# Start of a two-layer hybrid block: all of x loaded first, on the queue of the modulation weights, with the first dense weights between the two modulation vectors and x stored behind the modulation

## The chip, the cores and the metric

The kernel runs on one core of one Trainium2 chip. The metric is the device time of one execution in microseconds (us). The engines are named as the profile names them: PE (TensorE, the matmuls), PEld (its weight loads), DVE (VectorE), ACT (ScalarE), POOL (GpSimd) and SP (SyncE, here only a queue from which transfers are issued). SPq and ACTq are the queues on which SP and ACT issue transfers.

## The reference

Two layers work on 512 latent tokens and 256 context tokens of 1024 channels. Each begins with a normalization whose result is scaled and shifted by vectors computed from the conditioning input, and one wide input projection:

```python
def reference(x, c, ctx, c_ctx, ada_w, ada_b, norm1_w, norm2_w, w_in, w_out, ...):
    for l in range(DEPTH):
        mod_x = jnp.split((jax.nn.silu(c) @ ada_w[l] + ada_b[l])[:, None, :], N_MOD, axis=-1)
        mod_c = jnp.split((jax.nn.silu(c_ctx) @ ada_w[l] + ada_b[l])[None, None, :], N_MOD, axis=-1)
        hx = modulate(rmsnorm(x, norm1_w[l]), mod_x[0], mod_x[1])
        hc = modulate(rmsnorm(ctx, norm1_w[l]), mod_c[0], mod_c[1])
        mix_x, mix_c = token_mixing(hx, hc, w_in[l], ...)
        x = x + mod_x[2] * (mix_x @ w_out[l])
        x = x + mod_x[5] * channel_mlp(modulate(rmsnorm(x, norm2_w[l]), mod_x[3], mod_x[4]), ...)
        ...
    return rmsnorm(x, final_norm_w)
```

`token_mixing` multiplies by `w_in` and runs four groups of heads on the columns: a gated delta rule, windowed attention, a gated MLP over chunks, and a bidirectional mLSTM.

## The kernel before, in words

Everything is float32. The 768 tokens (context first) lie along the free axis: `X[k]` is a tile of 128 channels by 768 tokens, k = 0 to 7. Each dense matmul is made of three (`hhi*whi`, `hlo*whi`, `hhi*wlo`), for which ACT rounds a weight block to `whi`, DVE makes the rest `wlo`, and likewise `hhi` and `hlo` of the activations.

The start, up to the first dense matmul, does this. ACT issues the loads of the six blocks of 128 tokens (`xs`, 512 KB each, line 400) and takes their sums of squares (`jk`); PE transposes them (`xps`, line 406), and DVE and ACT copy the transposes to `X` (lines 184 and 412). SP issues the loads of the modulation weights (`adw`, line 323, 512 KB each, eight for each vector, in five buffers); PE multiplies them into `adaps`. Two vectors, n = 0 (shift) and n = 1 (scale), are needed at the start. `ada_end` copies a finished sum to `adas` on ACT, has PE turn it (`adat`) and DVE add the bias (`mod`). `params` loads a row of parameters (`prow`) and gate constants (`tokp`). `modulated` computes `sc` from the scale vector, then for each k on DVE `hy`, on ACT `hhi` and on DVE `hlo`. The first dense product (`gemm_pair`) works on two weight blocks together, 32 gate columns (two loads of 16 columns, 64 KB each) and 128 columns, both staged in `wst` by SP (line 491; two buffers) and split by `wsplit`. `X` is stored to DRAM (`xd`, line 628, eight transfers on ACT's queue) since its buffers are used for other things until the layer's residual.

The order of the instructions on each engine is not the order of the code: the framework's scheduler places each instruction by its own estimate of when it is ready. At the end of the layer's token mixing, a block named `mix0` (line 1513 on) weaves attention (`scl`, `scc`, `pT`, `pv`, `P`, `sq`), mLSTM (`W`, `wps`, `num`, `qk`, `hT`, `sT`, `den`, `hn`, `hs`, `lq`) and dense work, and is placed by such a simulated timeline too. After it the output projection begins with `mhi` and `mlo`, first of the tile `uu`.

Of the kernel before, what the change touches and what calls it, by code (L numbers as in the profile page):

```python
# [9 lines left out]
F32 = mybir.dt.float32  # L10
# [8 lines left out]
D = 1024  # L19
# [3 lines left out]
NP = NT // 128  # L23
DEPTH = 2
# [10 lines left out]
C_GQ, C_GK, C_GV, C_GZ, C_AB = 0, 256, 512, 768, 1024  # L35
C_SQ, C_SK, C_SV = 1040, 1296, 1424
C_MU, C_MV = 1552, 1808
C_LQ, C_LK, C_LV, C_LO, C_IF = 2064, 2320, 2576, 2832, 3088
# [104 lines left out]
def flow_kernel(ctx, tc, t, out, dbg=None, stop=None):  # L143
    nc = tc.nc
# [23 lines left out]
    def gi(name="gi"):  # L168
        return pg.tile([128, 512], F32, tag="gi", name=name)

    def go1(name="go"):
        return pg.tile([128, 512], F32, tag="go", name=name)
# [126 lines left out]
    lay, zp, tp = layer_pools()  # L299
    ldx = ExitStack()  # L300
    ld = ldx.enter_context(tc.tile_pool(name="ld", bufs=5))

    sg = ld.tile([128, 16], F32, name="csg", bufs=1)
    cv = ld.tile([128, 16], F32, name="cv", bufs=1)
# [14 lines left out]
    def ada_sum(l, n, pl, o):  # L319

        for k in range(8):
            st = pl.tile([128, 4, 256], F32, tag="adw", name="adw")
            nc.sync.dma_start(out=st, in_=t["ada_w"][l, 128 * k:128 * k + 128, 1024 * n:1024 * n + 1024]
                              .rearrange("p (g n) -> p g n", g=4))
            for g in range(4):
                mm(o[32 * g:32 * g + 32, 0:256], scT[:, k], st[:, g], start=(k == 0), stop=(k == 7))
        return o
# [67 lines left out]
    X = [xm.tile([128, NT], F32, tag="xm", name="x") for _ in range(8)]  # L395
    ss0 = per.tile([128, NP], F32, name="ss0")
    for p in range(NP):
        xs = ld.tile([128, D], F32, tag="xs", name="xs", bufs=6)
        src = t["ctx"][0, 128 * p:128 * p + 128] if p < 2 else t["x"][0, 128 * (p - 2):128 * (p - 2) + 128]
        nc.scalar.dma_start(out=xs, in_=src)  # L400
        jk = ld.tile([128, D], F32, tag="jk", name="jk", bufs=1)
        act_(jk, xs, AF.Square, accum_out=ss0[:, p:p + 1])
        for g in range(2):
            pt = ps("xps")
            for k in range(4):
                T.transpose(pt[:, 128 * k:128 * k + 128], xs[:, 128 * (4 * g + k):128 * (4 * g + k) + 128], ident)
            for k in range(4):
                xo = X[4 * g + k][:, 128 * p:128 * p + 128]
                if k % 2:
                    act_(xo, pt[:, 128 * k:128 * k + 128], AF.Copy)  # L410
                else:
                    V.tensor_copy(out=xo, in_=pt[:, 128 * k:128 * k + 128])

    nc.scalar.dma_start(out=cst[:, 128:], in_=t["consts"][:, 128:NPERM])


    prm = [per.tile([128, 128], F32, name=f"prm{l}") for l in range(DEPTH)]
    tokp = [per.tile([128, 44], F32, name=f"tokp{l}") for l in range(DEPTH)]

    def params(l, rows):  # L420
        nc.scalar.dma_start(out=rows[0:NR], in_=t["prow"][l])
        nc.scalar.dma_start(out=tokp[l], in_=t["tok"][l:l + 1].to_broadcast([128, 44]))
        pt = gs("prmT")[:, 0]
        T.transpose(pt[:, 0:NR], rows[0:NR, :], ident[0:NR, 0:NR])
        V.tensor_copy(out=prm[l][:, 0:NR], in_=pt[:, 0:NR])

    ao = [ada_sum(0, 0, ld, go1("adaps")), ada_sum(0, 1, ld, gi("adaps"))]
    params(0, ld.tile([128, 128], F32, tag="prow", name="prow", bufs=1))
    for n in range(2):
        ada_end(0, n, ld, ao[n])  # L430

# [47 lines left out]
        return parts  # L479

    def wload(parts, order=None):
        st = wst.tile([128, 8, 128], F32, tag="wst", name="wst")
        o = 0
        for src in parts:
            n = src.shape[1]
            sv = src.rearrange("(k p) n -> p k n", p=128)
            for i in (range(0, 8, 2) if order else (0,)):
                if order:
                    nc.sync.dma_start(out=st[:, i:i + 2, o:o + n], in_=sv[:, order[i]:order[i] + 2])
                else:  # L490
                    nc.sync.dma_start(out=st[:, :, o:o + n], in_=sv)
            o += n
        return wsplit(st, o)

    def gemm(parts, acts, segs, n=128, order=None, pb=None, w2=None):

# [103 lines left out]
    for l in range(DEPTH):  # L600
# [19 lines left out]
        def z3(name, dt=F32):  # L620
            return zp.tile([128, NT], dt, tag="z3", name=name, bufs=6)

        ahead = [wload([win[:, C_AB:C_AB + 16], win[:, C_IF:C_IF + 16]]), wload([win[:, C_GK:C_GK + 128]])]
        h = modulated(l, 0, ALL, nrm, tp)
        del nrm
        xd = dp.tile([8, 128, NT], F32, tag="xd", name="xd")
        for k in range(8):
            nc.scalar.dma_start(out=xd[k, :, ow], in_=X[k][:, ow])

        def temp(tag, w=GAP + 4):  # L630
            return tp.tile([128, GAP + 4], F32, tag=tag, name=tag, bufs=1 if tag == "tc" else 2)
# [881 lines left out]
        with tc.block(name=f"mix{l}", schedule_with_timeline_sim=True):  # L1513
            for _ in states():
                pass
            if l == 0:
                params(1, temp("tc")[:, 0:128])
            no = len(opairs)
            for j in range(2):
                gdn_norm(j)  # L1520
            weave((3.5 * no, swa()), (2 * no, mlstm()), (14, dense()))
            for j in range(2):
                mv = mix[6 + j][:, ow]
                tt(mv, mv, gz[j][:, ow], MUL)
# [112 lines left out]
```

## Time and profile before

| what | value |
|---|---|
| time, median of 3 runs (lowest to highest) | 1961.99 us (1960.19 to 1962.09) |
| the profiled execution | 1955.14 us |
| its span, first to last instruction | 1953.4 us |
| PE busy | 1874.8 us, 96% of the span |
| DVE, ACT busy | 1201.8 us, 757.4 us |

The profiled execution is 1.7 us longer than its span and 6.9 us below the median of the others. The profile cuts the span into slices in which each engine's busy share, the clock granted to TensorE (as a share of its full 2.4 GHz; 0.50 is 1.2 GHz) and the transfers' rate can be read; a chain of waits leads back from the last instruction.

### The profile page before, as it was taken

The numbers are of one execution on the slowest core, as the hardware profiler recorded it, in microseconds if no ns is written. First come the engines' busy times: TensorE is split into PE (matmuls) and PEld (weight loads), VectorE is DVE, ScalarE is ACT, GpSimd is POOL, SyncE is SP. The second block draws the span as 40 slices with busy tenths as digits, with TensorE's granted clock in tenths as the row PEclk, the third lists the DMA queues.
The fourth block names the chain that finished last, engine by engine and source line by source line (L and its number), as shares of the span: only waits on it lengthen the run. The fifth ranks groups of instructions, "written<-read, shape, count | busy, mean of one in ns | idle before, by whom it ended". The sixth has DMA issues, their size and how long they took to land.

```text
span 1953.4 us, 34015 instructions
## 1 busy us (share of the span) xinstructions
PE 1874.8 (96%) x14131; PEld 1536.4 (79%) x14131; DVE 1201.8 (62%) x2221; ACT 757.4 (39%) x1530; POOL 104.6 (5%) x169
## 2 busy tenths in 40 slices
PE   5999999999899999999999999999999999999998
PEld 3877778778777888888888878677777778888887
DVE  3978885666769557435535349798676754444443
ACT  4652343555524312313213236434255543333242
POOL 0021110000000000000000000211100000000001
PEclk8999999999799999999999999999999999999999
DMA  8321001121464345335433222210011323333332
GB/s 310 97 52 34 13 24 34 57 65 34 147 199 129 107 131 148 116 93 151 140 87 108 78 58 55 63 35 24 23 44 33 102 81 98 97 97 97 97 97 76
DMA packets 225955, 172.56 MB, mean 88 GB/s; under 512 B 19106, under 2 KB 208008, under 8 KB 225800
## 3 DMA queue, kind: packets, MB, share of 16 engines
q1 hardware_dynamic: 219424, 153.71, 26.6%
q10 hardware_dynamic: 4680, 10.64, 1.5%
q0 software_dynamic: 1696, 6.03, 0.9%
q8 instruction: 111, 1.82, 0.4%
q14 instruction: 44, 0.36, 0.1%
HBM read 163.02 MB, written 7.34 MB: 87 GB/s over the span
## 4 chain that ended last, share of the span: by engine, by line
PE 82%; DVE 9%; ACT 3%; DMA 3%; issue 1%; POOL 1%; DVEq 0%; ACTq 0%; SPq 0%; POOLq 0%
PE mm L181 64%; PE mmt L181 3%; PE num L181 1%; PE ops L181 1%; DMA wst<-w_in 1%; PE pv L181 1%; DVE wlo L187 1%; DVE Y L187 1%; PE adaps L181 1%; PE yt L181 1%; DVE kq L190 1%; PE t L181 1%; PE pT L1353 1%; DMA adw<-ada_w 1%; PE yps L181 1%
## 5 line engine op out<-in xcount | busy, mean ns | idle before, releaser
L184 ACT ACTIVATE whi<-wst 128x512 fp32r<-128x512 f32 (+1 forms) x388 | 241.9, 627 | 683.8 <-PE mm L181 628.8
L181 PE MATMUL mm<-hhi,whi 128*128 128x512 f32 (+3 forms) x1344 | 479.5, 362 | 11.7 <-ACT hhi L184 11.0
L181 PE MATMUL mm<-hlo,whi 128*128 128x512 f32 (+3 forms) x1344 | 479.3, 357 | 1.2 <-DVE hlo L190 1.1
L181 PE MATMUL mm<-hhi,wlo 128*128 128x512 f32 (+3 forms) x1344 | 476.3, 356 | 0.0
L187 DVE TENSOR_TENSOR wlo<-wst,whi 128x512 fp32r<-128x512 f32 (+1 forms) x388 | 265.7, 689 | 312.9 <-ACT whi L184 308.5
L181 PEld LDWEIGHTS mm<-hhi,whi 128*128 128x128 f32 (+1 forms) x1344 | 252.7, 189 | 55.2 <-ACT hhi L184 14.4
L181 PEld LDWEIGHTS mm<-hlo,whi 128*128 128x128 f32 (+1 forms) x1344 | 253.9, 189 | 38.0 <-DVE hlo L190 2.3
L181 PEld LDWEIGHTS mm<-hhi,wlo 128*128 128x128 f32 (+1 forms) x1344 | 253.2, 189 | 38.6 <-issue 1.5
L181 PE MATMUL mm<-fhi,whi 128*128 128x512 f32 (+1 forms) x784 | 275.9, 352 | 0.0
L181 PE MATMUL mm<-flo,whi 128*128 128x512 f32 (+1 forms) x784 | 275.8, 352 | 0.0
L181 PE MATMUL mm<-fhi,wlo 128*128 128x512 f32 (+1 forms) x784 | 274.5, 350 | 0.0
L190 DVE SCALAR_TENSOR_TENSOR x<-mm,mod,x 128x256 f32<-128x256 f32 (+1 forms) x122 | 79.6, 653 | 139.8 <-PE mm L181 139.7
L181 PEld LDWEIGHTS mm<-fhi,whi 128*128 128x128 f32 x784 | 148.3, 189 | 21.9 <-ACT r L184 0.8
L181 PEld LDWEIGHTS mm<-fhi,wlo 128*128 128x128 f32 x784 | 148.1, 189 | 19.7
L181 PEld LDWEIGHTS mm<-flo,whi 128*128 128x128 f32 x784 | 148.4, 189 | 19.1
L190 DVE SCALAR_TENSOR_TENSOR adacc<-adw,scT,adacc 128x1024 f32<-128x1024 f32 x84 | 105.9, 1282 | 28.0 <-DMA adw<-ada_w 27.9
L187 DVE TENSOR_TENSOR flo<-r,fhi 128x768 fp32r<-128x768 f32 (+1 forms) x64 | 52.6, 825 | 39.2 <-ACT fhi L184 39.1
L184 ACT ACTIVATE fhi<-r 128x768 fp32r<-128x768 f32 (+1 forms) x64 | 47.2, 740 | 65.9 <-DVE r L187 65.9
L181 PE MATMUL mm<-mlo,whi 128*128 128x512 f32 (+1 forms) x192 | 69.7, 363 | 1.3 <-DVE mlo L187 1.3
L181 PE MATMUL mm<-mhi,whi 128*128 128x512 f32 (+1 forms) x192 | 69.5, 362 | 0.4 <-ACT mhi L184 0.4
L181 PE MATMUL mm<-mhi,wlo 128*128 128x512 f32 (+1 forms) x192 | 68.8, 359 | 0.0
L184 ACT ACTIVATE r<-mm 128x256 f32<-128x256 f32 (+1 forms) x96 | 49.1, 515 | 32.2 <-PE mm L181 32.2
(406 smaller groups left out, 2712.1 us busy)
## 6 DMA issues: line engine op xcount, KB each, us to landing
wst<-mlp_w SPq DMA_DIRECT2D x128, 512.0 KB, 3.8
adw<-ada_w SPq DMA_DIRECT2D x96, 512.0 KB, 4.1
wst<-w_in SPq DMA_DIRECT2D x44, 512.0 KB, 3.7
wst<-w_out SPq DMA_DIRECT2D x64, 128.0 KB, 3.2
xd<-x ACTq DMA_DIRECT2D x8, 384.0 KB, 3.4
x<-xd POOLq DMA_DIRECT2D x8, 384.0 KB, 5.5
xs<-x ACTq DMA_DIRECT2D x4, 512.0 KB, 7.2
wst<-w_in SPq DMA_DIRECT2D x8, 256.0 KB, 3.2
```

What stands on the lines that cost most here:

```text
L181: T.matmul(o, lhsT=l, rhs=r, start=start, stop=stop)
L184: S.activation(out=o, in_=i, func=f, **kw)
L187: (eng or V).tensor_tensor(out=o, in0=a, in1=b, op=op)
L190: V.scalar_tensor_tensor(out=o, in0=a, scalar=s, in1=b, op0=op0, op1=op1)
L1353: T.transpose(o[:, 256 * i + 128 * g:256 * i + 128 * g + 128], Ps[g][:, 128 * (i0 + i):128 * (i0 + i) + 128], ident)
```

## The change

The six loads of context and x go to the front of SP's queue, ahead of the modulation weights. `prow`, `tokp` and the constants are issued at once on ACT's queue. The first two dense blocks are staged (`wstage`, the loading half of the former `wload`) between the loads of the two modulation vectors and split later. Before the eight stores of `X`, a transfer of eight numbers of the scale vector (`mod`) is written to the place they will overwrite, so that the stores come behind the modulation. `params` of layer 1 loads its rows where it did before, through the new `params_load`.

```diff
+    xin = []
+    for p in range(NP):
+        xs = ld.tile([128, D], F32, tag="xs", name="xs", bufs=6)
+        src = t["ctx"][0, 128 * p:128 * p + 128] if p < 2 else t["x"][0, 128 * (p - 2):128 * (p - 2) + 128]
+        nc.sync.dma_start(out=xs, in_=src)
+        xin.append(xs)
...
+    def params_load(l, rows):
+        nc.scalar.dma_start(out=rows[0:NR], in_=t["prow"][l])
+        nc.scalar.dma_start(out=tokp[l], in_=t["tok"][l:l + 1].to_broadcast([128, 44]))
+        return rows
+
+    prow = params_load(0, ld.tile([128, 128], F32, tag="prow", name="prow", bufs=1))
+    nc.scalar.dma_start(out=cst[:, 128:], in_=t["consts"][:, 128:NPERM])
+
+    def wstage(parts, order=None):
+
+        st = wst.tile([128, 8, 128], F32, tag="wst", name="wst")
...
+    def first_blocks(l):
+        win = t["w_in"][l]
+        return [[win[:, C_AB:C_AB + 16], win[:, C_IF:C_IF + 16]], [win[:, C_GK:C_GK + 128]]]
...
-        xs = ld.tile([128, D], F32, tag="xs", name="xs", bufs=6)
-        src = t["ctx"][0, 128 * p:128 * p + 128] if p < 2 else t["x"][0, 128 * (p - 2):128 * (p - 2) + 128]
-        nc.scalar.dma_start(out=xs, in_=src)
+        xs = xin[p]
...
-    ao = [ada_sum(0, 0, ld, go1("adaps")), ada_sum(0, 1, ld, gi("adaps"))]
-    params(0, ld.tile([128, 128], F32, tag="prow", name="prow", bufs=1))
+    params(0, prow)
+    ao = [ada_sum(0, 0, ld, go1("adaps"))]
+    staged = [wstage(x) for x in first_blocks(0)]
+    ao.append(ada_sum(0, 1, ld, gi("adaps")))
...
-        ahead = [wload([win[:, C_AB:C_AB + 16], win[:, C_IF:C_IF + 16]]), wload([win[:, C_GK:C_GK + 128]])]
+        ahead = [wsplit(*x) for x in staged] if l == 0 else [wload(x) for x in first_blocks(l)]
...
+        if l == 0:
+
+            nc.scalar.dma_start(out=xd[:, 0:1, 0].rearrange("k p -> p k"), in_=mod[0][0:1, 8:16, 0])
         for k in range(8):
             nc.scalar.dma_start(out=xd[k, :, ow], in_=X[k][:, ow])
```

What stands where changes on every engine at the start, and, since the scheduler runs again, in the last quarter of `mix0`. Three places matter below.

SP at the start of the program, before (`xs` is the input by tokens, `adw` the modulation weights, `wst` the staged dense weights):

```order
L197 DMA crow<-crow 16x128
L323 DMA adw<-ada_w 128x1024 x5
L491 DMA wst<-w_in 128x8x16
L323 DMA adw<-ada_w 128x1024 x11
L491 DMA wst<-w_in 128x8x16
L491 DMA wst<-w_in 128x8x128
```

The same place now:

```order
L197 DMA crow<-crow 16x128
L306 DMA xs<-ctx 128x1024 x2
L306 DMA xs<-x 128x1024 x4
L359 DMA adw<-ada_w 128x1024 x8
L330 DMA wst<-w_in 128x8x16 x2
L330 DMA wst<-w_in 128x8x128
L359 DMA adw<-ada_w 128x1024 x8
```

The input stands ahead of all modulation weights, and the three loads of the first dense weights, one of which stood between the first and two behind the last of them, stand between the vectors.

ACT at the end of the first dense product, before (`ta` is the copy of the product out of PSUM, `Re` a constant table):

```order
L184 ACTIVATE whi<-wst 128x512 x2
L184 ACTIVATE Re<-e__1150 64x512
L184 ACTIVATE hhi<-hy,mod_121 128x256
L184 ACTIVATE hhi<-hy,mod_121 128x512
L184 ACTIVATE ta<-mm 32x256
L184 ACTIVATE whi<-wst 128x512
L184 ACTIVATE ta<-mm 32x512
```

The same place now:

```order
L184 ACTIVATE hhi<-hy,mod_141 128x256
L184 ACTIVATE hhi<-hy,mod_141 128x512
L649 DMA xd<-x 128x768 x2
L184 ACTIVATE ta<-mm 32x256
L184 ACTIVATE ta<-mm 32x512
L184 ACTIVATE whi<-wst 128x512 x2
L184 ACTIVATE ta<-mm 128x256
```

The first two roundings of the next weight block, which stood ahead of the last `hhi`, stand behind two copies of the finished product; `Re` went to the start of the product, behind its first `hhi`.

DVE at the end of `mix0` and the start of the output projection, before:

```order
L187 TENSOR_TENSOR hs<-hs,ss 128x256
L1339 RECIPROCAL sm<-sm 128x2
L1342 TENSOR_SCALAR P<-P,sm 128x256 x2
L187 TENSOR_TENSOR lq<-lq,gz_4708 128x768
L187 TENSOR_TENSOR lq<-lq,gz_4709 128x768
L1364 COPY sq<-pv 128x128
L1513 UNCONDITIONAL_BRANCH
L649 TENSOR_SCALAR tokp_268<-tokp_268 128x8
L187 TENSOR_TENSOR mlo<-uu,mhi 128x768 x2
```

The same place now:

```order
L1385 COPY sq<-pv 128x128
L1504 TENSOR_REDUCE ss<-sq_6396 128x4
L187 TENSOR_TENSOR hs<-hs,ss 128x256
L1385 COPY sq<-pv 128x128
L187 TENSOR_TENSOR lq<-lq,gz_4709 128x768
L187 TENSOR_TENSOR lq<-lq,gz_4710 128x768
L1534 UNCONDITIONAL_BRANCH
L670 TENSOR_SCALAR tokp_126<-tokp_126 128x8
L187 TENSOR_TENSOR mlo<-uu,mhi 128x768 x2
```

The two products with the gate `gz` moved behind the last attention copy, to the end of the block.

## Rows read from the trace of the kernel before

**Rows 1.** The page: span of the profiled execution.

```profile
span 1953.4 us, 34015 instructions
```

**Rows 2.** Busy time by stretch (PE, PEld, DVE, ACT, POOL), then granted clock, DMA share, GB/s.

```profile
2.00:4.00 2.00, 0.26 (x1) 0.18 (x1) 1.15 (x8) 0.03 (x1) 0.00 (x0) 1.00 0.87 202
...
4.00:12.00 8.00, 4.39 (x24) 3.43 (x28) 1.60 (x8) 3.56 (x10) 0.00 (x0) 1.00 1.02 406
12.00:16.00 4.00, 4.00 (x41) 1.84 (x34) 1.03 (x5) 2.45 (x9) 0.00 (x0) 1.00 1.04 309
16.00:32.00 16.00, 9.58 (x73) 5.78 (x71) 3.02 (x11) 6.36 (x18) 0.00 (x0) 0.75 1.00 395
...
34.00:36.00 2.00, 2.00 (x19) 1.30 (x17) 0.00 (x0) 0.59 (x2) 0.00 (x0) 0.91 0.15 42
...
44.00:51.00 7.00, 4.80 (x15) 3.04 (x16) 6.93 (x14) 3.96 (x8) 1.52 (x5) 0.50 0.95 301
```

**Rows 3.** Timeline, 0 to 45 us, SP's queue: start, duration, what, count.

```profile
12.62 21.09 SPq L323 DMA_DIRECT2D adw<-ada_w  x11
33.75 1.09 SPq L491 DMA_DIRECT2D wst<-w_in  x2
```

**Rows 4.** Waits of SP's queue to 43 us: total us, times, longest.

```profile
SPq L323 <- PE adaps L181: 17.8, 7, 5.6
```

**Rows 5.** Transfers issued before 43 us: count, size each, median us to landing.

```profile
adw<-ada_w SPq DMA_DIRECT2D x16, 512.0 KB, 7.0
xs<-x ACTq DMA_DIRECT2D x4, 512.0 KB, 7.2
...
cst<-consts ACTq DMA_DIRECT2D x1, 512.0 KB, 7.6
wst<-w_in SPq DMA_DIRECT2D x1, 512.0 KB
cst<-consts ACTq DMA_DIRECT2D x1, 444.5 KB, 5.4
wst<-w_in SPq DMA_DIRECT2D x2, 64.0 KB, 8.6
```

**Rows 6.** Timeline of PE, 40 to 48 us: the last vector and the first dense matmul.

```profile
40.45 0.64 PE L181 MATMUL adaps<-adw,scT 128*32 128x256 f32 x8 [1.83 <-DMA adw<-ada_w]
...
45.93 0.42 PE L181 MATMUL mm<-hhi,whi 128*32 128x256 f32 x1 [3.32 <-ACT hhi L184]
```

**Rows 7.** The chain of waits, 28 to 70 us: the first dense product.

```profile
47.90 17.80 PE mm L181 x92
```

**Rows 8.** Timeline of DVE, 42 to 49 us: from the scale vector to the first `hlo`.

```profile
42.65 0.17 DVE L187 TENSOR_TENSOR mod<-adat,prm 128x16 f32<-128x16 f32 x1 [0.22 <-PE adat L181]
43.22 0.49 DVE L187 TENSOR_TENSOR wlo<-wst,whi 128x128 fp32r<-128x128 f32 x2 [0.40 <-ACT whi L184]
43.63 0.64 DVE L254 TENSOR_SCALAR sc<-mod 128x16 f32<-128x16 f32 x1
...
44.51 1.54 DVE L190 SCALAR_TENSOR_TENSOR hy<-x,sc,rstd 128x256 f32<-128x256 f32 x3
45.97 1.47 DVE L187 TENSOR_TENSOR wlo<-wst,whi 128x512 fp32r<-128x512 f32 x2
47.37 1.53 DVE L190 SCALAR_TENSOR_TENSOR hlo<-hy,mod,hhi 128x256 fp32r<-128x256 f32 x3
```

**Rows 9.** Timeline of ACT at the end of the first dense product.

```profile
64.69 0.63 ACT L184 ACTIVATE whi<-wst 128x512 fp32r<-128x512 f32 x1
```

**Rows 10.** Busy time by stretch at the end of `mix0`, columns as in rows 2.

```profile
488.00:495.00 7.00, 7.00 (x68) 5.80 (x66) 5.19 (x14) 5.68 (x13) 0.00 (x0) 1.00 0.00 0
495.00:499.00 4.00, 1.11 (x6) 0.52 (x5) 3.81 (x10) 3.99 (x15) 0.00 (x0) 0.95 0.00 0
499.00:511.00 12.00, 11.89 (x56) 10.12 (x56) 5.62 (x20) 2.10 (x6) 0.00 (x0) 0.50 0.01 1
```

**Rows 11.** Timeline of DVE at the end of `mix0`: the products with the gate.

```profile
514.40 1.89 DVE L187 TENSOR_TENSOR lq<-lq,gz 128x768 f32<-128x768 f32 x2 [0.24 <-ACT lq L184]
```

More of the change, by code (lines that the diff above doesn't have):

```diff
@@ L301, in flow_kernel @@
     ld = ldx.enter_context(tc.tile_pool(name="ld", bufs=5))
+    xin = []
[4 more added lines that the diff above has]
+        xin.append(xs)
+    prm = [per.tile([128, 128], F32, name=f"prm{l}") for l in range(DEPTH)]
+    tokp = [per.tile([128, 44], F32, name=f"tokp{l}") for l in range(DEPTH)]
+    def params_load(l, rows):
[6 more added lines that the diff above has]
+        st = wst.tile([128, 8, 128], F32, tag="wst", name="wst")
+        o = 0
+        for src in parts:
+            n = src.shape[1]
+            sv = src.rearrange("(k p) n -> p k n", p=128)
+            for i in (range(0, 8, 2) if order else (0,)):
+                if order:
+                    nc.sync.dma_start(out=st[:, i:i + 2, o:o + n], in_=sv[:, order[i]:order[i] + 2])
+                else:
+                    nc.sync.dma_start(out=st[:, :, o:o + n], in_=sv)
+            o += n
+        return st, o
+    def first_blocks(l):
+        win = t["w_in"][l]
+        return [[win[:, C_AB:C_AB + 16], win[:, C_IF:C_IF + 16]], [win[:, C_GK:C_GK + 128]]]
     sg = ld.tile([128, 16], F32, name="csg", bufs=1)
@@ L412, in flow_kernel @@
                     V.tensor_copy(out=xo, in_=pt[:, 128 * k:128 * k + 128])
-    nc.scalar.dma_start(out=cst[:, 128:], in_=t["consts"][:, 128:NPERM])
-    prm = [per.tile([128, 128], F32, name=f"prm{l}") for l in range(DEPTH)]
-    tokp = [per.tile([128, 44], F32, name=f"tokp{l}") for l in range(DEPTH)]
     def params(l, rows):
-        nc.scalar.dma_start(out=rows[0:NR], in_=t["prow"][l])
-        nc.scalar.dma_start(out=tokp[l], in_=t["tok"][l:l + 1].to_broadcast([128, 44]))
         pt = gs("prmT")[:, 0]
@@ L481, in wload @@
     def wload(parts, order=None):
[L482 to L493, printed above, removed]
+        return wsplit(*wstage(parts, order))
     def gemm(parts, acts, segs, n=128, order=None, pb=None, w2=None):
@@ L1516, in flow_kernel @@
             if l == 0:
-                params(1, temp("tc")[:, 0:128])
+                params(1, params_load(1, temp("tc")[:, 0:128]))
             no = len(opairs)
```

## The prediction

> **What bounds the kernel now.** I read the span first [rows 1], then busy time by stretch [rows 2], then, for the start, SP's queue, its waits and the transfers [rows 3 to 5], and last the chain from the last vector into the first dense product [rows 6 to 8]. PE is busy for 96% of the span and hardly ever idle outside the start, so a change that only reorders transfers can win at the start alone. There the transfers are the limit: from 4 to 32 us all sixteen DMA engines are full, at 406, 309 and 395 GB/s [rows 2]. Then comes a hole: 42 GB/s from 34 to 36 us. The reason is on SP's queue. It waits 17.8 us in seven waits for PE to release `adw` buffers [rows 4], because PE, in order, stands before transposes of x blocks that are still on their way; so the last load of the second vector is issued only at the end of the eleven that take from 12.62 to 33.71 us [rows 3], with two weight loads behind it at 33.75. The last vector reaches PE at 40.45 and the first dense matmul starts at 45.93 [rows 6]. From 47.90 the first product runs without a gap for 17.80 us [rows 7] and dense work follows. Whatever brings 47.90 forward is won in full, if nothing later gives it back.
>
> **Loads: what is moved.** Nothing is removed but the wait; the bytes stay the same, and their order changes. Ahead of the last vector now lie: 16 `adw` and 6 `xs` (four of x, two of context) of 512 KB (0.524 MB each, 11.53 MB), two tables of 512 and 444.5 KB (0.98 MB), the staged weights, 512 KB and two of 64 KB (0.66 MB) [rows 5], and some 0.15 MB of small ones: 13.32 MB. By 4 us about 0.41 MB have moved (202 GB/s over 2 us), and the full engines move 400 GB/s, between 395 and 406 [rows 2]. So 4 + 12.91/0.400 = 36.3 us. The two 64 KB loads are dear: the stretch from 12 to 16 us, in which one of them ran, lost (400 - 309) x 4 = 0.36 MB, or 0.9 us [rows 2]; both now stand ahead of the last vector, 1.8 us. I take 38.1 us, between 36.7 (406 GB/s, one of the two hidden) and 39.5 (395 GB/s and a bubble where an `adw` waits for its buffer). Against 40.45 that is 2.3 us, with ends at 0.9 and 3.7.
>
> SP's order could spoil this: each `adw` waits for PE to release the buffer of the fifth before it, and three weight loads and the second vector stand behind that wait. Five buffers hold five times 1.31 us of transfer (0.524 MB at 400 GB/s); a release, an issue and a landing take less while the queue is full, since x is through PE before most of the vectors. So I count it at nothing; if that cover is gone it costs the old wait again (the second rival).
>
> What the Trainium skill says against this stands in this paragraph alone. Its page "DMA: Bandwidth & Descriptors", section "Bandwidth", puts the limit of transfers from HBM at about 358 GB/s for a core. An estimate by that figure: the 12.91 MB would take 36.1 us and the last vector would land after 40 us, no sooner than now, and the kernel would stay at about 1961 us. The trace does not agree for a core that runs alone: 406 GB/s stood for 8 us [rows 2], and by the measured rate the sum is the one above.
>
> **From the vector to the product.** Before, 5.48 us pass from the last vector on PE to the first matmul [rows 6]. In them DVE has `mod` ready at 42.82 but starts `sc` at 43.63 [rows 8], behind the `wlo` of gate weights that had just landed. These weights now land some 10 us earlier and are split while the second vector loads: 0.8 us saved. Then the `wlo` of the other block follows one `hy` instead of three, 1.54 us for three [rows 8], so the first `hlo` comes a further 1.0 us sooner. PE can't use all of that: its fourth matmul needs the second `hhi`, whose `hy` now stands behind that `hlo`. From the durations of rows 8: first `hy` at 44.51 - 2.3 - 0.8 = 41.4, `wlo` to 43.2, `hlo` to 43.7, `hy` to 44.4, `hhi` to 45.1. So dense work begins at about 45.1 instead of 47.90: 2.8 us won, vector and all. Its length I leave at 17.8 us: the clock was at 0.50 (1.2 GHz) from 44 to 51 us [rows 2] after PE had waited for the vector, and PE waits about 3 us there now as well. If the clock were full there, some 1.6 us more would be won: half of the 3.1 us from 47.90 to 51.
>
> **Small pieces.** The roundings of the next weights now stand behind the copies of the finished product on ACT. PE's next matmul needs them: two copies, one rounding of 0.63 us [rows 9] and its `wlo` (0.7 us, half of the pair in rows 8), of which PE covers most with the gate columns' transposes and its first matmuls. I take 0.5 us lost, between 0 and 1.5. `Re` stands behind the first `hhi` and waits for a table that SP issues only once the vectors are done, and the second `hhi` stands behind `Re`. DVE's `hlo` and `hy` (1.1 us) hide a quick landing, and the queue is nearly empty then, so nothing; landing like the small weight loads, in 8.6 us [rows 5], it would hold the product by 4 us (39.2 + 8.6 + 0.6 against 44.4). The eight-number transfer and the stores behind it wait for `mod` on ACT's queue; behind them there stand only `hhi`s, which come later anyway: nothing, at most the few tenths that an issue takes. `prow`, `tokp` and the tables in the first microseconds add no bytes. Start in all: 2.8 - 0.5 = 2.3 us won, ends -2 and 5.
>
> **The end of `mix0`.** The scheduler moved things there too, and this is the largest unknown. From 495 to 499 us PE works 1.11 of 4 us, and from 499 to 511 it is busy 11.89 us at a clock of 0.50, while the 7 us before ran at 1.00 [rows 10]. Now one `W` and eight `num` leave this tail for the dense work before it (`sT` and `hn` come earlier on DVE), which shortens it; against that the two products with the gate, 1.89 us [rows 11], follow the last attention copy and stand before `mlo`, where before they ran while PE finished. I take 1 us won: about 2.9 us less to do in the tail, 1.9 us more at its end. The ends come from the clock: if PE no longer waits and the clock stays at 1.00, half of 11.89 us, 6 us, is won; if it waits earlier and the 7 us before are done at 0.50 as well, 7 us are lost.
>
> **The rivals.** (a) The clock stays up at the end of `mix0`, or at the first product: 1961.99 - 2.3 - 6 = 1953.7, or 1957 with the first product alone. For it: the wait there is short and `sT`, for which PE waited, comes earlier. Against: the tail is still a chain of small steps over three engines. (b) The clock falls earlier: the wait for `sT` comes in the dense part before 488 us, and the following 7 us run at 0.50: 1961.99 - 2.3 + 7 = 1966.7, slower. It decides if PE idles there for as long as it does now from 495 to 499. (c) The last vector comes no sooner: SP still waits for PE's releases, since the vector matmuls stand in order behind transposes which wait for ACT's copies. ACT has 6 sums and 24 copies, and when it lags, the fifth buffer comes free late. Then the start wins only the 0.8 us before `sc` less the 0.5: 1961.99 - 0.3 - 1 = 1960.7. For it: 17.8 us of such waits now [rows 4]. Against: by then eleven loads are queued.
>
> **How the numbers follow.** The profiled execution would go from 1955.14 to 1951.8 us, 3.3 us less (2.3 + 1.0); it lies 6.9 us below the median of the runs, and I take the same difference off that: 1958.7. Chances: forecast 0.55, (a) 0.20, (b) 0.12, (c) 0.13. A measurement of this kernel can tell about 0.2%, 3.9 us, from no change, so faster begins below 1958.1. The forecast's own spread (1956 to 1961) gives 0.20 faster and 0.35 same; (a) is faster; of (b) 0.10 is slower and 0.02 same; (c) is 0.12 same and 0.01 slower. Faster 0.40, same 0.49, slower 0.11. The range runs from (a)'s 1953.5 to 1963.5, which leaves out the deeper half of (a) and most of (b).
>
> **What would show it.** In the profile of the changed kernel: transfers full until the last vector, with no hole like the one from 34 to 36 us; the last vector on PE at about 38.1 us; first dense matmul near 42.8, dense work from 45.1, product done near 62.9 where it was 65.7; a gap of about half a microsecond before the next product. At the end of `mix0`, the output projection at 515 instead of 518.7 us, and the stretch at 0.50 neither longer nor gone. I am wrong on the start if the last vector lands after 39.5 us or SP's waits for `adaps` stay near 17.8 us; on `mix0` if the granted clock falls at another place.

## The result, and the profile after

| | before | changed |
|---|---|---|
| time, median of five runs each (lowest to highest) | 1960.25 us (1960.08 to 1962.09) | 1975.66 us (1970.26 to 1977.31) |
| ratio, with its 95% interval | 1 | 1.0075 (1.0057 to 1.0094) |
| last vector matmul of the start on PE | 40.45 us | 50.60 us |
| first transpose of the gate columns, behind the first dense product | 65.6 us | 77.5 us |

The change makes the kernel 15 us slower; 1958.7 was forecast, with a range to 1963.5. Of the 15 us, 11.9 are there when the first dense product is done. What answers to [rows 2] are these stretches of the changed kernel, with the same columns: length, busy time of PE, PEld, DVE, ACT and POOL, then granted clock, DMA share and GB/s.

```profile
4.00:8.00 4.00, 1.67 (x8) 1.64 (x9) 0.01 (x1) 1.26 (x3) 0.00 (x0) 1.00 0.67 250
8.00:12.00 4.00, 2.01 (x10) 1.61 (x8) 0.00 (x0) 0.00 (x0) 0.00 (x0) 1.00 0.99 403
12.00:16.00 4.00, 0.89 (x4) 0.89 (x5) 1.42 (x7) 2.28 (x10) 0.00 (x0) 1.00 0.58 197
...
24.00:28.00 4.00, 4.00 (x20) 1.95 (x18) 1.84 (x8) 3.42 (x14) 0.00 (x0) 1.00 0.01 4
28.00:32.00 4.00, 4.00 (x38) 2.60 (x38) 0.85 (x4) 1.62 (x6) 0.00 (x0) 1.00 0.61 173
32.00:36.00 4.00, 2.05 (x32) 0.74 (x32) 0.00 (x0) 1.32 (x2) 0.00 (x0) 1.00 0.95 252
36.00:40.00 4.00, 1.25 (x12) 0.68 (x12) 0.60 (x3) 0.78 (x3) 0.00 (x0) 0.88 0.74 209
```

Look at the last column first. Before, it stood at 406, 309 and 395 GB/s from 4 to 32 us [rows 2]. Now it falls to 250 and 197, and from 24 to 28 us to 4 GB/s: for four microseconds next to nothing is loaded. Then look at DVE: it does nothing at all from 8 to 12 us. DVE's own timeline says what for (start, duration, line, operation, and in brackets the idle time before it and what ended it):

```profile
3.83 0.17 DVE L344 TENSOR_SCALAR csg<-cv 128x16 f32<-128x16 f32 x1
12.98 0.17 DVE L1295 TENSOR_SCALAR nsk<-tokp 128x4 f32<-128x4 f32 x1 [8.97 <-DMA tokp<-tok]
13.06 0.28 DVE L446 COPY x<-xps 128x128 f32<-128x128 f32 x1
...
21.96 0.23 DVE L477 CAST gmask_r<-cst 128x128 fp32r<-128x128 f32 x1 [4.63 <-DMA cst<-consts]
```

`nsk`, a 0.17 us step on four columns that is wanted by the attention much later, stands in DVE's order in front of x's first copy, since its input is now loaded at once and the scheduler reckoned it early. But `tokp`, 22 KB, lands 11.2 us after its issue at 1.78 us, in the crowd of the other loads; before, it was issued at 33.31 and landed 6.5 us later. DVE stands for 8.97 us, and 4.63 us more before the first cast of the mask table. Behind it stand its copies of x, behind those ACT's copies, behind those PE's transposes (a transpose waits until a tile of `xps` has been copied out), and behind those, on PE, the vectors' matmuls. ACT's first copy of x, and PE's wait for ACT's copies (total us, times, longest):

```profile
13.38 0.28 ACT L184 ACTIVATE x<-xps 128x128 f32<-128x128 f32 x1 [5.81 <-DVE x L446]
...
PE xps L440 <- ACT x L184: 9.1, 3, 5.1
```

SP's waits, which answer to [rows 4], show where that ends:

```profile
SPq L359 <- PE adaps L181: 16.2, 7, 10.8
SPq L306 <- DMA prow<-prow: 6.1, 1, 6.1
...
SPq L306 <- DMA xs<-ctx: 3.2, 1, 3.2
```

One wait of 10.8 us for a buffer of `adw` is the hole at 24 us. The second row is a thing of its own: a load of x waits 6.1 us until `prow`, which it doesn't read, has landed. The trace shows what links them. Eight semaphores tell of the landings of these loads, in turn, on both queues, and a load is issued only when the transfer that had its semaphore before has landed. The fourth load of x has the one of `prow`: the last of `prow` lands at 12.76 us, and the load is issued at 12.78. In the third row it is the third load of x, behind the first of context. So the four loads of x, meant to be first, are issued until 13.11 us. SP's queue, for [rows 3]:

```profile
2.13 10.98 SPq L306 DMA_DIRECT2D xs<-x  x4
13.15 18.35 SPq L359 DMA_DIRECT2D adw<-ada_w  x8
31.55 4.96 SPq L330 DMA_DIRECT2D wst<-w_in  x3
36.60 9.18 SPq L359 DMA_DIRECT2D adw<-ada_w  x8
```

The third row is the staged weights between the vectors: SP spends 4.96 us on three issues. The two of 64 KB take 0.43 and 1.14 us, and the last, of the 512 KB, alone 3.3:

```profile
33.21 3.29 SPq L330 DMA_DIRECT2D wst<-w_in  x1
```

Before, one load of 64 KB and the one of 512 KB took 1.09 us together [rows 3]. The first vector matmul of the kernel before, then the rows of PE in the changed kernel for [rows 6], with the first vector matmul and the last transposes of x, and the chain's row for [rows 7]:

```profile
11.47 2.66 PE L181 MATMUL adaps<-adw,scT 128*32 128x256 f32 x18
```

```profile
24.26 1.06 PE L181 MATMUL adaps<-adw,scT 128*32 128x256 f32 x2
...
28.17 0.95 PE L440 MATMUL xps<-cst,xs 128*128 128x128 f32 x4
...
50.60 1.08 PE L181 MATMUL adaps<-adw,scT 128*32 128x256 f32 x8 [0.21 <-DMA adw<-ada_w]
...
56.58 0.42 PE L181 MATMUL mm<-hhi,whi 128*32 128x256 f32 x1 [2.98 <-ACT hhi L184]
```

```profile
59.46 18.14 PE mm L181 x93
```

The first vector matmul comes at 24.26 (11.47 before), the last eight begin at 50.60, the product starts in full at 59.46 and lasts 18.14 us (17.80 before).

### The profile page after: what moved, and what is told of

Its sections match the earlier page's. It is cut to its first block, busy times and chain, and to the rows that moved or that the text cites. A ratio compares the mean times of both kernels' runs of the same rounds, so it can differ in the third digit from the quotient of the medians.

```text
span 1968.5 us, 34015 instructions
## 1 busy us (share of the span) xinstructions
PE 1880.7 (96%) x14131; PEld 1539.2 (78%) x14131; DVE 1201.9 (61%) x2221; ACT 755.5 (38%) x1530; POOL 104.2 (5%) x169
## 4 chain that ended last, share of the span: by engine, by line
PE 83%; DVE 8%; DMA 4%; ACT 3%; issue 1%; POOL 1%; DVEq 0%; ACTq 0%; SPq 0%; POOLq 0%
PE mm L181 64%; PE mmt L181 3%; DMA adw<-ada_w 2%; PE ops L181 1%; PE num L181 1%; PE adaps L181 1%; PE pv L181 1%; DVE Y L187 1%; PE yt L181 1%; PE t L181 1%; PE pT L1374 1%; DVE wlo L187 1%; PE yps L181 1%; PE scl L181 1%; PE rps L181 1%
## 5 line engine op out<-in xcount | busy, mean ns | idle before, releaser
L181 PE MATMUL mm<-hhi,whi 128*128 128x512 f32 (+3 forms) x1344 | 480.7, 362 | 11.9 <-ACT hhi L184 11.1
```

The lines of the kernel that those rows point to most:

```text
L181: T.matmul(o, lhsT=l, rhs=r, start=start, stop=stop)
```

## The experiments

The table has all of them; each ratio is against the kernel before, run in turn with it on the same chip. "Last vector" (where the last eight vector matmuls begin) and "gates" are the two places of the table above.

| kernel | last vector | gates | median, us | ratio (95% interval) |
|---|---|---|---|---|
| before | 40.45 | 65.6 | 1960.25 | |
| changed | 50.60 | 77.5 | 1975.66 | 1.0075 (1.0057 to 1.0094) |
| e12, changed again | 49.87 | 77.2 | 1975.01 | 1.0080 (1.0062 to 1.0097) |
| e1, `nsk` behind x | 43.05 | 69.3 | 1966.59 | 1.0033 (1.0016 to 1.0050) |
| e2, `nsk` and masks behind x | 45.31 | 73.1 | 1967.84 | 1.0031 (1.0017 to 1.0046) |
| e3, small loads late | 43.28 | 70.9 | 1966.24 | 1.0033 (1.0020 to 1.0046) |
| e4, before, small loads early | 43.54 | 69.1 | 1966.56 | 1.0030 (1.0013 to 1.0047) |
| e5, all consumers behind | 41.60 | 68.0 | 1963.70 | 1.0012 (0.9991 to 1.0033) |
| e6, and POOL's memsets held | 42.45 | 68.4 | 1961.54 | 1.0016 (1.0001 to 1.0031) |
| e7, before, memsets held | 40.38 | 64.9 | 1960.85 | 1.0001 (0.9988 to 1.0014) |
| e8, changed, stores not held | 55.72 | 82.2 | 1978.91 | 1.0098 (1.0061 to 1.0135) |
| e9, e5 unstaged | 38.71 | 65.0 | 1960.00 | 1.0004 (0.9994 to 1.0015) |
| e10, e9, masks between vectors, memsets held | 37.17 | 62.2 | 1956.55 | 0.9981 (0.9968 to 0.9995) |
| e11, before, stores and memsets held | 41.10 | 66.1 | 1960.88 | 1.0007 (0.9995 to 1.0019) |
| e13, e10, staged | 41.73 | 68.1 | 1964.98 | 1.0029 (1.0015 to 1.0044) |
| e14, changed, unstaged | 46.96 | 73.0 | 1967.93 | 1.0039 (1.0021 to 1.0058) |

**e1 and e2: the steps in front of x's copies.** A one-element copy from x's last block into the step's output makes the scheduler put the step behind x; the loads are left alone.

```diff
+        if l == 0:
+            V.tensor_copy(out=nsk[:, 0:1], in_=xlast)
         V.tensor_scalar(out=nsk, in0=tokp[l][:, 40:44], ...)
```

e2 does the same for the six casts of the mask table.

> The changed kernel with one thing undone: DVE's small step `nsk`, which reads `tokp`, is held behind x's last copy by a one-element write; all loads stay as changed. In the trace of the changed kernel DVE stands 8.97 us before `nsk` (until `tokp` lands at 12.96) and 4.63 us before the mask casts (until 21.96), with x's copies behind both. Theory A (these two stands on DVE hold x, x holds PE, PE holds the `adw` buffers): the second stand is still there, so the last vector comes at 47 to 50.6 us and the time is 1971 to 1976. Theory B (the bytes of x, the tables and the staged weights ahead of the second vector make it late, and DVE's stands are slack): last vector at 50 to 51, 1974 to 1977.

> As the run before, and the six casts of the mask table are held behind x's last copy as well, so that no small load stands before a copy of x on DVE; the loads are still issued at once. Theory A: x is through PE once it has landed, some 19 to 22 us, the hole in the transfers near 24 to 28 us closes, the last vector comes at 43 to 46 us, and the time is 1966 to 1971. Theory B: last vector at 49 to 51 and 1972 to 1977.

With `nsk` out of the way, the last vector comes 7.5 us sooner and the time falls by 8 to 9 us (by the ratios and by the medians). That is more than theory A had said, because the second stand goes with the first: the mask table's load is issued behind copies on ACT which had waited for DVE, now at 9.06 us instead of 14.02. DVE's timeline in e1, where x's first copy comes at 8.09 us instead of 13.06:

```profile
8.09 0.29 DVE L446 COPY x<-xps 128x128 f32<-128x128 f32 x1 [4.07 <-PE xps L440]
...
15.81 0.23 DVE L478 CAST gmask_r<-cst 128x128 fp32r<-128x128 f32 x1 [0.99 <-DMA cst<-consts]
```

Of 4.63 us, 0.99 are left, so that e2 had nothing more to win. It lands where it was expected to (45.31, 1967.84), but so would any run without the first stand: its time is e1's. That its last vector comes 2.3 us behind e1's was not explained.

**e3 and e4: the small loads themselves.** e3 issues them only when x has been copied; e4 adds the early small loads alone to the kernel before.

```diff
+    for d in (prow[0:NR, 0:1], tokp[0][:, 0:1], cst[:, 128:129]):
+        V.tensor_copy(out=d, in_=X[6][0:d.shape[0], NT - 1:NT])
+    nc.scalar.dma_start(out=cst[:, 128:], in_=t["consts"][:, 128:NPERM])
```

> The changed kernel with the part on the small loads undone: `prow`, `tokp` and the two tables are issued only after x's last copy (each destination is written once from x first), the rest stays as changed. Theory A, with the addition that the small loads also hold up the issue of x on SP (SP waits 6.1 us for `prow` before it issues x): both are gone, x has landed by about 12 to 14 us, the last vector comes at 38 to 41 us, dense work starts at 46 to 49 us, and the time is 1958 to 1965, with what is lost in the first mixer block (some 3 us) left. Theory B: the same bytes lie ahead of the last vector, so it comes at 45 to 50 us and the time is 1968 to 1975.

> The kernel before with only the small loads moved: `prow`, `tokp` and the 444.5 KB table are issued in the first microseconds; x stays on the ACT queue, no staged weights, stores as before. DVE's `nsk` and the copy of `prm` then stand before x's copies, the mask casts behind them. Theory A: DVE stands until `tokp` lands, about 11 to 13 us, `scT` and the first vector's matmuls come 2 to 4 us late, x's first buffers too: last vector at 42 to 46, 1962 to 1968. Theory B: these loads are no longer ahead of anything that matters, 1957 to 1961.

In e3 x is issued by 4.05 us and through PE at 16, and yet the last vector comes at 43.28: a new stand had taken the place of the old, this time on PE, whose transpose of `prow` the scheduler put between the vectors' matmuls. In e4 the same transpose stands in front of x. PE's timelines, e3 and then e4:

```profile
26.15 0.41 PE L454 MATMUL prmT<-cst,prow 107*128 107x107 f32 x1 [6.42 <-DMA prow<-prow]
```

```profile
10.89 0.44 PE L430 MATMUL prmT<-cst,prow 107*128 107x107 f32 x1 [7.91 <-DMA prow<-prow]
```

e4 says the more: nothing but the early small loads makes the kernel before 6 us slower. It lands in theory A's ranges, with the stand on PE for `prow` where the theory had put it on DVE for `tokp`. e3 decides less: 43.28 and 1966.24 lie between its two theories, since its own edit made another wait, and the staging, taken up below, is still in it.

**e5 and e9: no stands at all, and then no staging.** In e5, x goes first on SP, the small loads follow on SP, the masks' load lands behind the vectors, and `prm`'s transpose stands behind the first vector. e9 takes out the staged weights as well.

```diff
-    staged = [wstage(x) for x in first_blocks(0)]
...
-        ahead = [wsplit(*x) for x in staged] if l == 0 else [...]
+        ahead = [wload(x) for x in first_blocks(l)]
```

> The order of loads that the change aims at, without anything that stands on an in-order engine for a small load: x first on SP, then `prow`, `tokp` and the 444.5 KB table on SP behind x, then the vectors; the mask table's load on SP too, which the scheduler puts behind the last vector; `nsk` and the mask casts behind x's last copy (or later), and `prm`'s transpose on PE behind the first vector's matmuls. Theory A (what cost the time are loads that land late while an in-order engine stands for them, with x and the vectors behind): PE and DVE stand for no small load, the transfers stay full, the last vector comes at 37 to 39.5 us, dense work starts at 45 to 48.5, and the time is 1956 to 1962. Theory B (the bytes put ahead of the second vector make it late): it still comes at 42 us or later, as in the run with the small loads late (43.3), and the time is 1963 to 1968.

> The kernel of e5 (x first, small loads behind it, their consumers behind x) without the staged weights: the first dense weights are loaded behind the second vector, as before the change. In e5 SP stands 3.15 us in the issue of one of the two 64 KB loads, and the transfers fall to 76 GB/s from 26 to 28 us; its last vector came at 41.60. Theory F (the staged loads between the vectors cost SP's queue and the transfers what x first had won): the second vector is issued about 5 us sooner, the hole is gone, the last vector comes at 38.5 to 40 us; dense work then waits for its weights and starts at 46.5 to 48.5; 1959 to 1964. Theory G (the second vector is held by PE's releases or by bytes, not by the staged loads): last vector at 41 to 42 as in e5, dense work at 49 to 50, 1963 to 1967.

With no step standing for a small load, the last vector still comes 1.2 us later than before. That lies between theory A's 37 to 39.5 and theory B's 42 or more, and the time is within theory B's range, so something else of the change was still at work; the staging was what was left to take out. Without it the last vector comes at 38.71, and theory F holds. That this is near the 38.1 that had been forecast is chance: e9 has neither the staged weights nor the mask table ahead of its last vector, and the forecast counted both.

**e10, e13 and e14: the price of the staging.** e10 is e9 with the mask table loaded between the vectors and POOL's memsets held (below); e13 puts the staged weights back into e10; e14 takes them out of the changed kernel.

> As e9, and two small moves: the mask table (512 KB) is loaded between the two vectors, so that its casts don't stand between `sc` and hy, and POOL's memsets are held until the first product's copy. It tells what the table's bytes ahead of the second vector cost against the 0.9 us of casts behind the vector. Theory F: last vector 1.3 us later than in e9 (0.52 MB at 400 GB/s), 39.8 to 41.3; first hy 0.9 us closer to it; the time within 2 us of e9. Theory G: last vector at 42 or later.

> e10 with the staged weights put back between the vectors, nothing else changed: a price for that one part. In e10 the last vector came at 37.17 us and dense work began at 42.99. Theory F (the 64 KB loads between the vectors hold SP's queue some 3 us and run far under the full rate): last vector at 39.5 to 42, dense work 2 to 4 us later than in e10, 1959 to 1963 against 1956.6. Theory H (in e9 and e10 it was not the staging but where the mask table's load stands): last vector at 37 to 38.5 and dense work at 42.5 to 44, 1955 to 1958.

> The changed kernel without the staged weights, DVE's `nsk` still in front of x's copies. Theory A and F together: DVE stands until 13 us and the mask casts until 22, as in the changed kernel, SP's eight loads of the second vector are no longer behind the weight loads, so the last vector comes 2 to 4 us sooner than the 50.6 and 49.9 of the changed kernel, at 46 to 48.5, and the time is 1971 to 1974. Theory F alone (the staging were most of the loss): last vector at 42 or less, 1963 to 1966.

e13 against e10 is the one part alone: 4.6 us at the last vector, 5.9 at the gates, 8.4 in the medians, more than theory F had said (dense work 6.3 us later, 49.31 against 42.99, for an expected 2 to 4, and 1964.98 for at most 1963). e14 agrees from the other side: 3 to 3.6 us, 4.2 to 4.5, and 7 to 8 (each against both runs of the changed kernel), so that its time fell below the 1971 to 1974 that had been expected. The stretches from 24 to 28 us, e10 and then e13, show it:

```profile
24.00:26.00 2.00, 1.62 (x16) 0.40 (x16) 0.00 (x0) 0.00 (x0) 0.00 (x0) 0.50 1.00 401
26.00:28.00 2.00, 1.50 (x12) 0.72 (x5) 0.16 (x1) 0.38 (x1) 0.00 (x0) 0.50 1.00 404
```

```profile
24.00:26.00 2.00, 1.35 (x12) 0.20 (x8) 0.00 (x0) 0.00 (x0) 0.00 (x0) 0.50 1.02 222
26.00:28.00 2.00, 1.47 (x10) 0.59 (x11) 0.26 (x2) 0.82 (x3) 0.00 (x0) 0.50 0.54 105
```

Look at the last two columns. From 24 to 26 us the engines are as busy in both (1.02 and 1.00) and move half as much in e13: that is the 64 KB loads in 64-byte pieces, as the packets of these 2 us in e13 show.

```profile
DMA packets 1804, 0.44 MB, mean 222 GB/s; under 512 B 1725, under 2 KB 1725, under 8 KB 1803
```

From 26 to 28 they are half idle, because SP has been held in issuing the weights and hasn't issued the next vector. On SP's queue in e13 the three issues last 6.36 us, the last of them 3.63:

```profile
19.88 6.36 SPq L331 DMA_DIRECT2D wst<-w_in  x3
...
22.61 3.63 SPq L331 DMA_DIRECT2D wst<-w_in  x1
```

The expectations of e9 and e13 take the long issue for one of a 64 KB load. It is that of the 512 KB load right behind the two: 3.15 us in e5, 3.63 in e13, and 3.51 in e10 as well, where it comes behind the last vector's loads. What such an issue waits for, no run shows.

The rest, between vector and gates, fits `Re`, which stands in front of the second `hhi` on ACT and waits for its table (e13's ACT, where e10 has no such row before the product):

```profile
47.89 0.63 ACT L184 ACTIVATE Re<-e__1161 64x512 fp32r<-64x512 f32 x1 [1.32 <-DMA e__1161<-consts]
```

e10 was expected to have its last vector later than e9, for the 0.52 MB put ahead of it, and had it 1.5 us sooner, with a median 3.5 us lower. In e9 the table is issued right behind the last `adw`, which was still on its way; whether they shared the engines was not tried apart. e10 is also the only kernel that beats the kernel before: 3.4 us at the gates, ratio 0.9981.

**e8 and e11: the stores behind the modulation.** e8 is the changed kernel without the eight-number write; e11 is e7 with that write added.

```diff
-            nc.scalar.dma_start(out=xd[:, 0:1, 0].rearrange("k p -> p k"), in_=mod[0][0:1, 8:16, 0])
```

> The changed kernel without the eight-number write of `mod` into `xd` that keeps the stores of x behind the modulation: stores may start as early as before. Theory A: the vectors come as late as in the changed kernel (last one at 50 to 51 us), the stores share the transfers with nothing that is waited for or cost up to 1 us: 1972 to 1978, as the changed kernel. Theory E (the write, its issue on ACT's queue and the stores behind it cost time between the vector and the product): the distance from the last vector to dense work falls from 8.9 towards 7.5 us, and the time to 1971 to 1974.

> The kernel before with its loads as they are, POOL's memsets held (as e7), and of the change only the small write of `mod` that puts x's stores behind the modulation. In e8, the changed kernel without that write, the stores ran among the vectors and the last vector came at 55.7 us instead of 50.6. Before, one store (384 KB) is issued at 36.89, ahead of the landing of the last vector. Theory: without it the last vector comes up to 1 us sooner, 39.3 to 40.4, dense work at 46 to 47 instead of 47.9, the time 1957 to 1961, 0 to 3 us under before, which the times may not tell from nothing. Rival: the write, its issue (0.73 us) and the `hhi` behind it on ACT's queue cost as much: dense work at 47 to 48, 1960 to 1963.

In e8 all eight stores of x are issued between 26.26 and 41.2 us, since x is now early, in the middle of the vectors. SP waits for one of them, and the last vector comes 5.1 to 5.9 us later than in the two traces with the write:

```profile
SPq L330 <- DMA xd<-x: 5.3, 1, 5.3
```

So neither theory held: the write saves 5 us at the last vector. In the time that isn't shown, with four runs of e8 between 1972.48 and 1985.30 and intervals that overlap. The weight load that waits here reads nothing of x either: it has the semaphore of a store that lands at 35.75, and is issued at 35.77. In the kernel before the write has nothing to save (e11): only one store stood ahead of the vector's landing. Dense work begins 1.1 us later than in e7 (47.54 against 46.48), but this isn't the write: x's last transposes end as much later (33.78 against 32.70), before there is any store, and from `mod` to the product e11 takes 3.5 us where e7 takes 4.2. In the time nothing of it is seen (1960.88 and 1960.85).

**e6 and e7: `sc` and POOL's memsets.** In e7 the kernel before has one thing changed, a wait of POOL's three memsets on the first product.

```diff
+        if l == 0:
+            G.tensor_copy(out=Nl[0:32, 0, 0, 0:1], in_=zg[0:32, 0:1])
         for x in ATb + [Nl]:
             G.memset(x, 0.0)
```

> The run before this one, and POOL's three memsets of the first block (`gc`, `cb`, `Nl`), which start as the last vector is done, are held until the first product's copy. In all traces so far DVE's `sc`, 128x16, ends when POOL's memset of `Nl` ends: 0.64 us long where it starts late (43.63 to 44.27 against 44.23), 1.41 where it starts with the memsets (53.84 to 55.25 against 55.22). Theory C (DVE's `sc` can't go on while POOL runs its memsets): `sc` takes 0.2 us, and first hy and dense work come 1.2 us sooner than in the run before this one, 1 to 2 us in the time (under what the times can tell). Theory D (`sc` is slow for another reason, such as the reading of `mod` on ACT's queue at that time): `sc` stays at 1.4 us and nothing moves.

> The kernel before with only POOL's three memsets held until the first product's copy. Theory C: `sc` follows `mod` within 0.3 us unless `wlo` of the gates still comes first, takes 0.2 us instead of 0.64, dense work starts at 47.2 to 47.6 instead of 47.90; the time is within 2 us of before. It also gives a second trace of the kernel before from 66 us on: if the stage from the gates' transposes to the first matmul of the output projection, 453.1 us in its trace and 455 to 461 in those of the variants, is long because of the variants' order, it is 453 to 454 here as well; if it is the clock, it may be anything from 453 to 461.

e6 couldn't tell: in e5, the kernel that it was made from, the memsets already came behind `sc`, which took 0.17 us in both. In e7 it could. DVE in the changed kernel, POOL in the changed kernel, and DVE in e7:

```profile
53.64 0.17 DVE L187 TENSOR_TENSOR mod<-adat,prm 128x16 f32<-128x16 f32 x1 [14.48 <-PE adat L181]
53.84 1.41 DVE L254 TENSOR_SCALAR sc<-mod 128x16 f32<-128x16 f32 x1
```

```profile
54.26 0.96 POOL L789 MEMSET Nl<- 128x1024 f16 x1
```

```profile
42.79 0.17 DVE L254 TENSOR_SCALAR sc<-mod 128x16 f32<-128x16 f32 x1
```

`sc` goes from 0.64 us [rows 8] to 0.17, and the gates come 0.7 us sooner: theory C. Theory D's reading of `mod` on ACT's queue is in e11 too, and `sc` takes 0.17 us there. In the time it can't be seen (1.0001).

**e12 and the first mixer block.** e12 is the changed kernel once more.

> The changed kernel once more, to see what of its time and of its trace repeats. If DVE's two stands are the cause at the start, they are there again: `nsk` at 12 to 14 us, the first mask cast at 21 to 23, last vector at 49 to 52, dense work at 58 to 61. From the gates' transposes on (456.0 us to the output projection in the first trace, with 453.1 and 459.1 in two traces of the kernel before whose orders on PE, DVE and ACT are the same) it may be anything from 453 to 461 if the clock decides; if the changed order of the first mixer block costs 3 us, it is 455 to 457. Time 1972 to 1977.

All the marks of the start repeat. What doesn't is the stage from the gates to the output projection. Four stretches, from the gates to the first `mlo` matmul: before, e7, changed, e12.

```profile
65.60:518.70 453.10, 428.31 (x4444) 342.14 (x4443) 325.43 (x721) 211.06 (x492) 40.93 (x59) 0.96 0.14 40
```

```profile
64.90:524.00 459.10, 433.66 (x4444) 347.12 (x4443) 325.98 (x721) 210.92 (x492) 41.92 (x61) 0.95 0.14 40
```

```profile
77.50:533.50 456.00, 430.54 (x4444) 344.85 (x4443) 327.41 (x723) 211.06 (x493) 41.07 (x59) 0.96 0.14 39
```

```profile
77.20:536.70 459.50, 434.90 (x4444) 348.96 (x4443) 327.85 (x723) 211.16 (x493) 41.08 (x59) 0.95 0.14 39
```

The kernel before and e7 have the same order of instructions on DVE and ACT, and on PE but for one matmul, and yet 453.1 and 459.1 us, with a mean clock of 0.96 and 0.95; the changed kernel has 456.0 and 459.5. Executions of one order differ by as much as the two orders do, or more. So the changed order, `mix0` included, has no price that these traces show. It also fits that the profiled execution of before (1955.14) lay below the median of its runs: its stage was a short one.

## Why the prediction was wrong, point by point

- **What bounds the start.** Right for the kernel before: transfers are the limit. In the changed one they are not, from 24 to 28 us. What brings the dense work forward is won in the time: e10, with the gates 3.4 us sooner, is 3.7 us faster in the medians; the changed kernel, with 11.9 us lost, is 15 slower. The 3 us between are not settled; the stage from the gates to the output projection alone spreads by 6 us.
- **"`prow`, `tokp` and the tables in the first microseconds add no bytes."** This step failed, and most of the loss is here. The bytes were counted, and not the place of what reads them: `nsk` and the casts had moved in front of x's copies on DVE. Taking `nsk` away gave back 7.5 us at the last vector (e1); the loads alone make the kernel before 6 us slower (e4). The sum had no term for it, although the order was there to be read before any run. Nor had it one for the load of x that waits 6.1 us for `prow`.
- **"SP's order could spoil this ... so I count it at nothing."** Failed too, by its cover: "x is through PE before most of the vectors" was untrue, x being through PE at 29 us. Rival (c), the vectors' matmuls behind transposes that wait for copies, had the right mechanism. It blamed ACT's own work where ACT stood behind DVE, and priced it as a gain that doesn't come, 1960.7, where the last vector comes 10 us later: the wait is not bounded by the old one, as a load that lands late sets it. Its sign was there: SP waits 16.2 us for `adaps`, where 17.8 had been named as the mark of being wrong.
- **The staged weights: 0.66 MB, and 1.8 us for the two 64 KB loads.** The term was mis-sized: it comes to 3.4 us at 400 GB/s, and staged between the vectors the three loads cost 4.6 us at the last vector and 5.9 at the gates (e13 against e10). Their thin transfers had been read from the stretch 12 to 16 us of [rows 2]; that SP can stand over 3 us in one issue, with a whole vector behind it, had not, since before the change two were issued in 1.09 us [rows 3]. The Trainium skill's page "DMA: Bandwidth & Descriptors", section "Specifications", asks for pieces of 512 bytes or more for the full rate; the 64 KB loads have 64, and e13's 222 GB/s with full engines, beside e10's 401, agrees.
- **The last vector at 38.1 us.** The sum fell short even without the stands. e13 has the forecast's own bytes ahead of the last vector and none of the stands, and it comes at 41.73, behind 39.5. In e10, without the staged weights, the same sum gives 34.6 us (an estimate: 12.25 MB at 400 GB/s from 4 us on), and 37.17 were measured. Of these 2.6 us some 1.7 can be read off e10: in the three microseconds from 10 to 13, while `prow`, `tokp` and the 444.5 KB table are on their way, it moves 279, 131 and 89 GB/s, 0.70 MB less than at 400. The rate itself held elsewhere. The Trainium skill's page "DMA: Bandwidth & Descriptors", section "Bandwidth", names about 358 GB/s for a core when both cores of an HBM domain stream, and 425 GB/s measured for one transfer of 16 MB with the other core idle. e10's 401 and 404 GB/s are nearer the second figure, which the prediction had left out.
- **0.8 us before `sc`.** Not won. The `wlo` was moved away as foreseen, but `sc` then took 1.41 us and ended with POOL's memset: 1.44 us behind `mod`, where before it was 1.45 [rows 8].
- **`Re` behind the first `hhi`, counted as nothing, up to 4.** It waited 0.5 us in the changed kernel and 1.3 in e13, and took 0.63 itself: within the bound, not nothing.
- **The eight-number write and the stores: nothing.** Right on the cost. From `mod` to the product in full it is 5.8 us with the write (changed) and without it (e8). That the stores would otherwise run among the vectors once x is early, 5 us at the last vector, was not foreseen.
- **The first product's 17.8 us** was 18.14: right. **`mix0`, 1 us won, and rivals (a) and (b):** the granted clock does fall at another place: it is at 0.50 from 521 us on, some 443 behind the gates, where before it fell at 499 [rows 10], 433 behind them. But in e7, with the order of before, it fell 439 us or more behind the gates too, and no run shows a gain or a loss from the order, as the stage differs by 6 us between executions of one order.

## What to carry to other kernels

Before a load is moved forward, look up on every in-order engine what reads it: if a scheduler puts the reader by an estimate of the landing, a step of 0.2 us can hold an engine for as long as the slowest small load takes in a full queue. An early load wants its reader tied to a late place; e10 does that with one-element copies. That doesn't undo all of an early load's cost: e10's transfers still dip while the small loads land. And a row of weight loads in small pieces belongs where its queue has nothing urgent behind it, since an issue can stand as well as a transfer.

## What the runs showed of the hardware

- A 22 KB load landed in 6.5 us when it was issued at 33 us and in 11.2 us among the loads of the first microseconds; 53.5 KB of `prow` held PE for 7.91 us in e4.
- A transfer's issue can wait for a landing that it doesn't use: 6.1 us for `prow` before a load of x, 5.3 us for a store of x before a weight load (e8). In both the later transfer has the semaphore of the earlier one.
- Of three weight loads issued in a row, 64, 64 and 512 KB, the issue of the third kept SP for 3.3 us in the changed kernel, 3.63 in e13 and 3.51 in e10; before, behind one of 64 KB, it took 0.61. The issue of `tokp`, 22 KB, took 0.37 us before and 3.97 in e13, right behind `prow` and six loads of x and context.
- A DVE step of 0.17 us took 1.41 us beside POOL's memsets and ended 0.03 us behind the one shown. The Trainium skill's page "SBUF — State Buffer", section "SBUF: two separate sides", says that a GpSimd operation and a DVE operation in a two-port mode share a pair of ports, which the one that starts first holds for its whole instruction while the other stands. The two rows fit that, and e7, with the memsets held, has 0.17 us; which mode `sc` runs in, no run here shows.
